# Where the sums of the output projection's weights and rows are formed: GpSimd inside the last two attention runs, VectorE beside the products

## The chip, the cores and the metric

The kernel runs on one core of one Trainium2 chip. The metric is the device time of one execution in microseconds. The kernel before was timed three times: 1077.59, 1077.86 and 1077.87 us, median 1077.86 us. One more execution was taken with the profiler; its time was 1078.45 us and its span in the trace 1076.5 us, so 1.95 us lie outside the span. All start times below count from the start of that span.

## The reference

One layer of a bidirectional encoder over 2048 tokens of width 1024. The token grid is 32 rows of 64 columns; attention is two-dimensional neighbourhood attention (8 rows by 16 columns around a query) with a learned bias per head.

```python
h = rmsnorm(x, norm_0)
proj = h @ w_in_0                      # (2048, 1024) @ (1024, 4096)
q, k, v, gate = jnp.split(proj, 4, axis=-1)
o = neighbourhood_attention(q, k, v, rpb_0)    # 16 heads of 64
x = x + (o * jax.nn.silu(gate)) @ w_out_0      # (2048, 1024) @ (1024, 1024)
return rmsnorm(x, norm_f)
```

Everything is float32. A product is made of three matmuls on a high part and a low part of each operand: high by high, high by low, low by high. Forming the parts of a 128x512 tile takes a copy on ScalarE (the high part, rounded) and a subtraction on VectorE (the low part).

## The kernel before, in words

**Stages.** First come the projections of v, q, k and the gate. Then 32 attention runs follow (16 heads in 8 pairs, by 4 blocks of 8 grid rows), with projection work and later the first output tiles fed between them as filler for TensorE. In run m the kernel normalises and transposes the weights of attention of run m-1, issues the scores of run m and then the products with v of run m-1. The loop goes to m = 32, where no new scores are issued. After it the rest of the output projection runs alone, and only this end of the program, from about 935 us on, is touched by the change.

**The output projection.** The 16 row tiles of 128 tokens are the result's units. Tiles 0 to 7 are made plainly, inside the runs (matmuls of lines 1332 to 1336). Tiles 8 to 15 are made in four pairs, (8,9), (10,11), (12,13) and (15,14), after the runs, in `rows_by_seven`: a pair of row tiles and the two halves of K and of the output columns form a 2x2 by 2x2 block product, done in seven block products instead of eight (Winograd's form of Strassen's scheme). This needs sums of blocks on both sides:

- weights: T1, T2, T3 and T4 from the four quarters B11, B12, B21, B22 of `w_out`. `land_first` and `land_rest` load the quarters again as raw tiles (16 DMAs, line 1354), `sum_T1` and `sums_T23` form T1 to T3 on GpSimd (lines 1369, 1373, 1374), `sum_T4` on VectorE (1378), and `split_quarter` makes their high and low parts (ScalarE 1389, VectorE 1390).
- rows: for each pair A11, A12, A21, A22 are loaded by `load_rows_of` (line 1401). `sum_rows` forms S1 to S4 on GpSimd (line 1413), and `form_rows` makes high and low parts (ScalarE 1406, VectorE 1407).

**The seven products.** Each product is 12 matmuls 128x128 by 128x512 (line 1432). The order in a pair is P1, P6, P2, P7, P5, P4, P3; for the first two pairs P1 and P2 of both are put in front: P1(8,9), P1(10,11), P2(8,9), P2(10,11), then the other five of the first pair, then of the second. Products share PSUM banks: P2 adds onto the bank of P1, P7 and P4 onto that of P6, P3 onto that of P5. So P2 must wait until ScalarE has copied P1 out (line 1437), P7 until VectorE has read P6 (line 1442), P4 until VectorE has read P7 (1442), P3 until VectorE has read P5 (line 1213). GpSimd adds the residual rows to some of these intermediate tiles (lines 1445, 1449).

**Closing a row tile.** `add_rows` adds the residual (1213), `square` sums squares on ScalarE (1216), `finish` takes the root and scales: inside the runs the root is a polynomial of eight small VectorE instructions (1236 to 1243), after the runs VectorE, ScalarE's square root and VectorE again (1231 to 1234); then two multiplications on VectorE (1251) and two stores (1255). The last tile, 15, has its own form (1199 to 1209, 1227, 1247, 1248).

**What sets the order.** The order on each engine is the order in which the program issues instructions; each engine works through its own queue strictly in that order. All loads and most stores are issued by SyncE's queue, also in order. A clock counted in matmuls (`due`, `store`, `later`) decides when a deferred step is issued; in `rows_by_seven` the table `todo` attaches loads, sums and splits to the index of a product.

## Time and profile before

| what | value |
|---|---|
| median of three timed runs | 1077.86 us |
| the profiled execution | 1078.45 us, span 1076.5 us, mean granted clock 0.985 |
| TensorE busy (matmuls) | 1045.8 us, 97% |
| VectorE busy | 733.3 us, 68% |
| ScalarE busy | 556.1 us, 52% |
| GpSimd busy | 312.9 us, 29% |
| last matmul of the attention products ends | 965.35 us |
| last matmul of all ends | 1068.88 us |

How to read it: a timeline row gives start, duration, engine, line, operation, output and input tiles, count, and in brackets how long the engine had been idle and which instruction released it. A row with a count merges neighbours: its duration is from the first start to the last end. In a stretch view "PEclk" is the TensorE clock that was granted, 1.00 being full speed. Matmul ends overlap the next start, so the pace of matmuls is read from their starts.

### The profile page before, as it was taken

The page shows a single profiled execution, that of the slowest core. Times are in us where ns is not written, and L with a number is a line of the kernel's source. Part 1 is how long each engine was busy: PE and PEld are TensorE (multiplying, and loading weights), DVE is VectorE, ACT ScalarE, POOL GpSimd, SP SyncE. Part 2 cuts the span into 40 slices and gives each one's busy share as a digit, 9 for nine tenths or more (in the row PEclk, how much of TensorE's full clock was granted, in tenths as well). Part 3 has the DMA queues.
Part 4 walks back from the last instruction along what each step waited for, and adds up shares of the span by engine and source line. Part 5 has one row for each costly group of instructions (what it writes and reads, how often), then busy time and mean ns, then how long its engine had stood idle before and what let it go on. Part 6 is the DMA issues. An engine that isn't in the chain of part 4 may idle for free. (4 is left out here: it accounts for less than half of the span.)

```text
span 1076.5 us, 20235 instructions
## 1 busy us (share of the span) xinstructions
PE 1045.8 (97%) x7268; PEld 854.9 (79%) x7268; DVE 733.3 (68%) x1569; ACT 556.1 (52%) x1299; POOL 312.9 (29%) x382
## 2 busy tenths in 40 slices
PE   9999999999999999999999999999999999995896
PEld 6888888887888888888887888888887888874685
DVE  5475667768897535564656665777877877679566
ACT  7645233434453333333323777787887766554233
POOL 0000312212220000000003677665654322264462
PEclk9999999999999999999999999999999999987899
DMA  9634444444455334342327778778776897781542
GB/s 315 213 98 130 131 139 136 130 136 148 147 166 147 89 88 122 94 127 99 117 87 242 234 237 251 216 260 241 250 236 208 257 300 258 243 276 53 166 137 78
DMA packets 123708, 188.51 MB, mean 175 GB/s; under 512 B 11160, under 2 KB 55448, under 8 KB 123608
## 3 DMA queue, kind: packets, MB, share of 16 engines
q1 hardware_dynamic: 123176, 186.83, 55.6%
q8 instruction: 57, 0.93, 0.3%
q10 hardware_dynamic: 432, 0.40, 0.1%
q14 instruction: 43, 0.35, 0.1%
HBM read 136.85 MB, written 50.33 MB: 174 GB/s over the span
## 5 line engine op out<-in xcount | busy, mean ns | idle before, releaser
L436 PE MATMUL pp<-h,f 128*128 128x512 f32 x672 | 217.3, 389 | 0.0
L1042 ACT ACTIVATE x<-x,st 128x360 f32<-128x360 f32 (+5 forms) x256 | 151.2, 593 | 23.0 <-DVE st L1036 23.0
L436 PEld LDWEIGHTS pp<-h,f 128*128 128x128 f32 x672 | 126.1, 188 | 26.1
L1056 POOL TENSOR_SCALAR x<-x,st 128x480 f32<-128x480 f32 (+5 forms) x192 | 112.2, 602 | 117.1 <-DVE st L1047 113.9
L436 PE MATMUL pp<-t,f 128*128 128x512 f32 x558 | 141.7, 389 | 0.1
L456 POOL TENSOR_TENSOR tmp<-tmp,rb 128x512 f32<-128x512 f32 x36 | 58.4, 1622 | 268.8 <-DVE tmp L454 233.4
L436 PE MATMUL pp<-l,f 128*128 128x512 f32 x336 | 130.7, 389 | 0.0
L996 POOL TENSOR_TENSOR em<-e,mk 128x264 f32<-128x264 f32 (+3 forms) x64 | 50.9, 827 | 260.3 <-DMA mk<-in_masks_dram 246.8
L1036 DVE CUSTOM_DVE_ANT_0 x<-s,em 128x360 f32<-128x360 f32 (+5 forms) x256 | 122.9, 535 | 0.0
L436 PEld LDWEIGHTS pp<-t,f 128*128 128x128 f32 x558 | 104.7, 188 | 22.3 <-DVE u L449 0.6
L419 DVE TENSOR_TENSOR f<-raw,f 128x512 fp32r<-128x512 f32 x105 | 76.5, 729 | 43.6 <-ACT f L418 43.5
L1028 PE MATMUL s<-kt,q 64*128 64x480 f32 (+5 forms) x512 | 94.6, 487 | 0.3 <-ACT k L366 0.3
L1135 PEld LDWEIGHTS o<-pta,vt 120*64 120x64 f32 (+2 forms) x1792 | 81.8, 138 | 16.1 <-DVE st L1036 13.6
L560 PE MATMUL pv<-wh,h 128*128 128x512 f32 x256 | 88.4, 390 | 0.7 <-ACT h L521 0.4
L1135 PE MATMUL o<-pta,vt 120*64 120x128 f32 (+5 forms) x1792 | 86.4, 254 | 2.2 <-ACT pta L1089 1.8
L560 PE MATMUL pv<-wl,h 128*128 128x512 f32 x256 | 88.2, 390 | 0.0
L560 PE MATMUL pv<-wh,l 128*128 128x512 f32 x256 | 88.1, 389 | 0.0
L1028 PEld LDWEIGHTS s<-kt,q 64*128 64x128 f32 x512 | 64.9, 186 | 15.8 <-DVE pta L1089 1.1
L418 ACT ACTIVATE f<-raw 128x512 fp32r<-128x512 f32 x105 | 63.7, 624 | 26.5 <-PE pp L436 12.5
L1089 DVE COPY pta<-ph 120x512 f32<-120x512 f32 (+5 forms) x96 | 56.9, 639 | 29.6 <-PE ph L1113 29.5
L436 PEld LDWEIGHTS pp<-l,f 128*128 128x128 f32 x336 | 63.1, 188 | 13.2
L1089 ACT ACTIVATE pta<-ph 120x512 f32<-120x512 f32 (+5 forms) x96 | 49.6, 557 | 38.0 <-PE ph L1113 37.3
(192 smaller groups left out, 1903.4 us busy)
## 6 DMA issues: line engine op xcount, KB each, us to landing
raw<-in_wg_dram SPq DMA_DIRECT2D x124, 256.0 KB, 4.3
row<-in_xr_dram SPq DMA_DIRECT2D x32, 256.0 KB, 4.2
vd<-v SPq DMA_DIRECT2D x32, 256.0 KB, 2.6
sgd<-sg SPq DMA_DIRECT2D x32, 256.0 KB, 2.4
q<-qd SPq DMA_DIRECT2D x32, 256.0 KB, 5.5
sgt<-sgd SPq DMA_DIRECT2D x32, 256.0 KB, 6.2
xr<-in_x_dram SPq DMA_DIRECT2D x32, 256.0 KB, 5.1
ogd<-og SPq DMA_DIRECT2D x32, 256.0 KB, 3.3
```

The source lines that it names most:

```text
L418: nc.scalar.activation(t[:, 0], src, AF.Copy)
L419: nc.vector.tensor_tensor(t[:, 1], src, t[:, 0].bitcast(F32), OP.subtract)
L436: nc.tensor.matmul(B[n, P], t[:, int(m == 2), c], x[k][int(m == 1)], start=P in (1, 6, 5) and k == 0 and m == 0, stop=k == 3 and m == 2, s ...
L456: nc.gpsimd.tensor_tensor(tmp, tmp, rb[c], OP.mult)
L560: nc.tensor.matmul(ps[t], a[:, o], b, start=k == 0 and m == 0, stop=k == NK - 1 and m == 2)
L996: (nc.gpsimd if attending[0] or not s else nc.vector).tensor_tensor(sh(t), E[p, s][:, u0 + 4:u1 + 4, v0 + 8:v1 + 8].rearrange("p u (s v) - ...
L1028: nc.tensor.matmul(pst[s], qt[a, qs], kt[a, :r1 - r0, c0:c1].rearrange("p r (s c) -> p s r c", c=8), start=True, stop=True)
L1036: nc.vector.tensor_tensor_reduce(X[i, C][s], pst[s], EM[p, ROW_TYPE[T], COL_TYPE[C], s], -1.0, 1e38, OP.add, OP.min, st[:, o:o + 1])
L1042: nc.scalar.activation(X[i, C][s], X[i, C][s], AF.Exp, bias=st[:, o:o + 1], scale=-1.0, accum_out=st[:, 4 + o:5 + o])
L1056: nc.gpsimd.tensor_scalar(X[i, C][s], X[i, C][s], st[:, o:o + 1], 1.0, op0=OP.mult, op1=OP.mult)
L1089: (nc.vector.tensor_copy if h else lambda o, i_: nc.scalar.activation(o, i_, AF.Copy))(t[:k, h, b * 512:b * 512 + w], banks_[b, h][:k, :w])
L1135: nc.tensor.matmul(to.rearrange("d (h q) -> d h q", q=64) if nq > 64 else to, vt[:k, strip, s * 64:s * 64 + 64], t[:k, h, at:at + 64] if n ...
```

## The change

The constant `PLAIN` stays 8, so that in the new code `E` is 2 and the order of the products, and of all matmuls, is as before. What differs:

1. **Weights' sums.** One more raw quarter (B22's third) is loaded with the first ten, and all eleven are issued in one go in run 31, not one after another over several matmuls. `sum_T1` is issued in run 31 before its scores; the first two of the eight T2/T3 sums at the end of run 31, the other six in run 32 where all twelve stood. All are still on GpSimd.
2. **Rows' loads.** A11 and A12 of the first two pairs are loaded in run 31 instead of 32; the other row and residual loads are placed anew in `todo`.
3. **First splits.** The high and low parts for P1 of the two first pairs are issued before the transposes of run 32, those for P2 after them, where before all four stood after.
4. **Rows' sums** S1 to S4 move from GpSimd to VectorE for all four pairs; S4 overwrites S2 and not A12.
5. **Splits of T1, T3, T4 and the T4 sum** are issued after the fourth, first, sixth and first product; before, T3 and the T4 sum stood ahead of all products, T1 after the first and T4 after the second.
6. **Roots.** Tile 7, whose root came after the runs, now takes the polynomial form on VectorE; ScalarE's square root comes first with tile 9.
7. **Tile 14** is multiplied by the final norm's weights before its root is known, like tile 15, and scaled by ScalarE and VectorE half each.

```diff
+        if n == tiles - 2:
+            w = ev([128, 512], F32, "yw")
+            nc.vector.scalar_tensor_tensor(w, y, 0.5 ** 0.5 / NF_SCALE, late["nf"][j], op0=OP.mult, op1=OP.mult)
+            Y[n][0][j] = w
         store(("y", n, j), 5, square)
...
-            if ended[0]:
+            if n >= PLAIN:
                 nc.vector.tensor_scalar(h, st[:, 0:1], st[:, 1:2], 0.5 * D * EPS, op0=OP.add, op1=OP.add)
                 nc.scalar.activation(h, h, AF.Sqrt)
                 nc.vector.reciprocal(r, h)
-                nc.vector.tensor_scalar(r, r, 0.5 ** 0.5 / NF_SCALE, None, op0=OP.mult)
+                if n < tiles - 2:
+                    nc.vector.tensor_scalar(r, r, 0.5 ** 0.5 / NF_SCALE, None, op0=OP.mult)
                 return
...
-            if n == tiles - 1:
+            if n >= tiles - 2:
                 nc.scalar.activation(y[0], y[0], AF.Copy, scale=r)
                 nc.vector.tensor_scalar(y[1], y[1], r, None, op0=OP.mult)
...
-            store(("y", n), 24, scale)
+            store(("y", n), 12 if n == tiles - 2 else 24, scale)
...
-        which = [(f, k) for f in ("B12", "B11") for k in range(4)] + [("B22", 0), ("B22", 1)]
+        which = [(f, k) for f in ("B12", "B11") for k in range(4)] + [("B22", k) for k in range(3)]
...
-        A[m, f] = xp([128, 512], F32, "s") if f in ("S1", "S2") else A[m, {"S3": "A21", "S4": "A12"}[f]]
-        nc.gpsimd.tensor_tensor(A[m, f], A[m, a], A[m, b], o)
+        A[m, f] = xp([128, 512], F32, "s") if f in ("S1", "S2") else A[m, {"S3": "A21", "S4": "S2"}[f]]
+        nc.vector.tensor_tensor(A[m, f], A[m, a], A[m, b], o)
...
-            U[m, 1] = ep([128, 512], F32, "p1")
+            U[m, 1] = (xp if m == 2 else ep)([128, 512], F32, "p1")
...
-        for f in ("S1", "S2", "S3", "S4"):
-            sum_rows(0, f)
-        sum_T4()
+        for f in ("A21", "A22"):
+            load_rows_of(0, f)
+        for m in range(E):
+            load_rest_of(m, 0, 0)
         split_quarter("T2", [a[k, 1] for k in range(4) for a in (woh, wol)])
         sixth = sixths()
-        split_quarter("T3", [fresh(lp)] + [fresh(vh)] * 2 + [fresh(sp)] + sixth[:4])
         for i, (m, P) in enumerate(seq):
             rows_product(m, P)
             if i == 0:
+                sum_T4()
+                split_quarter("T3", [fresh(lp)] + [fresh(vh)] * 2 + [fresh(sp)] + sixth[:4])
+            if i == 3:
                 spot = mkp([128, 3, 512], F32R, "t1")
                 split_quarter("T1", [spot[:, j] for j in range(3)] + [fresh(kp, 960)] + sixth[4:6] + [fresh(vh)] * 2)
-            if i == 1:
+            if i == 5:
                 split_quarter("T4", [fresh(mp)] * 6 + [fresh(kp, 960), fresh(mp)])
...
-            later_loads(land_first(), 1, 0.7)
+            later_loads([lambda: [f() for f in land_first()]], 1.5, 0)
+            later_loads([lambda f=f, i=i: load_rows_of(i, f) for i in ((2, 0, 1) if PLAIN <= 6 else (0, 1)) for f in ("A11", "A12")], 10, 0.5)
         if m == cycles:
             later_loads([land_rest], 4, 0)
-            later_loads([lambda f=f, i=i: load_rows_of(i, f) for f in ("A11", "A12") for i in range(2)], 6, 0.5)
-            later_loads([lambda f=f: load_rows_of(0, f) for f in ("A21", "A22")], 10, 0.5)
...
             if m == cycles:
-                sum_T1()
-                sums_T23(range(2))
-                sums_T23(range(2, 4))
+                sums_T23(range(1, 4))
...
+        if m == cycles:
+            for n in range(3 if PLAIN <= 6 else 2):
+                form_rows(n, 1)
         sums = next_sums(m) == m + 1
         if m:
             turns(m - 1)
...
-            for s in ((0, 1), (1, 1), (0, 2), (1, 2)):
-                form_rows(*s)
+            for n in range(3 if PLAIN <= 6 else 2):
+                form_rows(n, 2)
         else:
+            if m == cycles - 1:
+                sum_T1()
             scores(2 * m)
...
             values(2 * m - 2)
             values(2 * m - 1)
+        if m == cycles - 1:
+            sums_T23((0,))
```

More of the change, by code (lines that the diff above doesn't have):

```diff
@@ L1358, in land_first @@
         homes = [spot[:, i] for i in range(3)] + [kp([128, 960], F32, "land")[:, :512]]
-        homes += [mp([128, 512], F32, "land") for _ in range(4)] + [qp([128, 512], F32, "land"), sp([128, 512], F32, "land")]
-        which = [(f, k) for f in ("B12", "B11") for k in range(4)] + [("B22", 0), ("B22", 1)]
+        homes += [mp([128, 512], F32, "land") for _ in range(4)] + [p([128, 512], F32, "land") for p in (qp, sp, lp)]
+        which = [(f, k) for f in ("B12", "B11") for k in range(4)] + [("B22", k) for k in range(3)]
         return [lambda w=w, h=h: load_quarter(*w, h) for w, h in zip(which, homes)]
     def land_rest():
-        for w in [("B22", 2), ("B22", 3)] + [("B21", k) for k in range(4)]:
+        for w in [("B22", 3)] + [("B21", k) for k in range(4)]:
             load_quarter(*w, mp([128, 512], F32, "land"))
@@ L1462, in rows_by_seven @@
             TF[f] = [(woh[4 * r + k, c], wol[4 * r + k, c]) for k in range(4)]
-        seq = [(0, 1), (1, 1), (0, 2), (1, 2)] + [(m, P) for m in (0, 1) for P in order7 if P not in (1, 2)]
-        seq += [(m, P) for m in range(2, len(PAIRS)) for P in order7]
+        E = 3 if PLAIN <= 6 else 2
+        seq = [(m, P) for P in (1, 2) for m in range(E)] + [(m, P) for m in range(E) for P in order7 if P not in (1, 2)]
+        seq += [(m, P) for m in range(E, len(PAIRS)) for P in order7]
         at = {s: i for i, s in enumerate(seq)}
@@ L1471, in rows_by_seven @@
         for i, s in enumerate(seq):
-            if i >= 4:
+            if i >= 2 * E:
                 on(i - 3, form_rows, *s)
         for m in range(len(PAIRS)):
-            s = at[m, 6] if m < 2 else at[m, 1]
-            first = s - (5 if m == 1 else 7)
-            if m:
-                if m == 1:
-                    names = ((first, "A21"), (first, "A22"))
-                else:
-                    names = ((first, "A21"), (first, "A22"), (first + 2, "A11"), (first + 3, "A12"))
-                for i, f in names:
-                    on(i, load_rows_of, m, f)
-                for i, f in ((2, "S1"), (2, "S2"), (2, "S3"), (3, "S4")) if m == 1 else ((4, "S1"), (4, "S2"), (5, "S3"), (7, "S4")):
-                    on(first + i, sum_rows, m, f)
-            for d, j, k in ((-2, 0, 1), (-2, 0, 0), (-1, 1, 1), (0, 1, 0)):
-                if m > 1:
-                    on(s + d, load_rest_of, m, j, k)
-                elif (j, k) != (0, 0) and (m, j, k) != (0, 0, 1):
-                    on(s + d, load_rest_of, m, j, k)
-        for f in ("S1", "S2", "S3", "S4"):
-            sum_rows(0, f)
-        sum_T4()
+            s = at[m, 6] - (m >= E)
+            loads = {0: (), 1: ((-7, "A21"), (-6, "A22")), 2: ((-7, "A21"), (-6, "A22"), (-6, "A11"), (-6, "A12"))}
+            for d, f in loads.get(m, ((-7, "A21"), (-7, "A22"), (-6, "A11"), (-4, "A12"))):
+                on(s + d, load_rows_of, m, f)
+            for d, f in ((-4, "S1"), (-4, "S2"), (-3 if m < E else -2, "S3"), (-2 if m < E else -1, "S4")):
+                on(s + d, sum_rows, m, f)
+            rest = ((-3, 1, 0), (-2, 0, 1), (-1, 1, 1)) if m == 0 else ((-3, 1, 0), (-3, 0, 1), (-2, 1, 1)) if m < E else                 ((-2, 0, 1), (-2, 0, 0), (-1, 1, 0), (0, 1, 1))
+            for d, j, k in rest:
+                on(s + d, load_rest_of, m, j, k)
+        for f in ("A21", "A22"):
+            load_rows_of(0, f)
+        for m in range(E):
+            load_rest_of(m, 0, 0)
         split_quarter("T2", [a[k, 1] for k in range(4) for a in (woh, wol)])
         sixth = sixths()
-        split_quarter("T3", [fresh(lp)] + [fresh(vh)] * 2 + [fresh(sp)] + sixth[:4])
         for i, (m, P) in enumerate(seq):
@@ L1653, in build @@
         due(1)
-    for e in ((0, 0, 0), (1, 0, 0), (0, 0, 1)):
-        load_rest_of(*e)
     rows_by_seven()
```

## The prediction

> **What bounds the kernel now.** I read the page's slices first: TensorE is at nine tenths nearly everywhere, except in slice 37 of 40, and its granted clock sinks there too.

> ```profile
> PE   9999999999999999999999999999999999995896
> ...
> PEclk9999999999999999999999999999999999987899
> ```

> Then the stretch view for TensorE alone (columns: stretch, length, busy, count, PEclk, DMA share, GB/s), the timelines of TensorE, ScalarE and GpSimd, and VectorE's.

> ```profile
> 959.00:963.00 4.00, 1.85 (x42) 1.00 0.96 305
> 963.00:970.00 7.00, 6.79 (x46) 0.52 0.90 333
> ...
> 977.00:986.00 9.00, 0.00 (x0) 0.50 0.00 0
> 986.00:990.00 4.00, 3.69 (x9) 0.50 0.00 0
> ...
> 1011.00:1015.00 4.00, 0.48 (x3) 0.94 0.47 169
> 1015.00:1021.00 6.00, 5.79 (x14) 0.50 0.50 171
> ```
> ```profile
> 961.18 0.66 PE L1135 MATMUL o<-pta,vt 96*64 96x128 f32 x8 [1.79 <-ACT pta L1089]
> 962.20 3.15 PE L1135 MATMUL o<-pta,vt 96*64 96x64 f32 x48 [0.36 <-DVE pta L1089]
> 965.56 0.80 PE L1432 MATMUL py<-woh,f 128*128 128x512 f32 x1 [0.21 <-ACT f L1406]
> ...
> 986.31 0.80 PE L1432 MATMUL py<-woh,f 128*128 128x512 f32 x1 [12.74 <-ACT p L1437]
> ...
> 997.63 1.61 PE L1432 MATMUL py<-t,f 128*128 128x512 f32 x6 [0.88 <-DVE u L1442]
> ...
> 1015.21 2.90 PE L1432 MATMUL py<-t,f 128*128 128x512 f32 x6 [3.73 <-ACT f L1406]
> ...
> 1020.46 1.95 PE L1432 MATMUL py<-t,f 128*128 128x512 f32 x6
> ...
> 1022.94 3.57 PE L1432 MATMUL py<-t,f 128*128 128x512 f32 x15
> ...
> 1026.35 0.39 PE L1432 MATMUL py<-woh,f 128*128 128x512 f32 x1
> ...
> 1068.49 0.39 PE L1432 MATMUL py<-woh,f 128*128 128x512 f32 x1
> ```
> ```profile
> 974.53 1.71 POOL L1413 TENSOR_TENSOR s<-raw 128x512 f32<-128x512 f32 x1
> ```
> ```profile
> 977.33 1.28 ACT L1232 ACT_TABLE_LOAD   x1
> 985.57 0.20 ACT L1232 ACTIVATE st<-st 128x1 f32<-128x1 f32 x1 [6.96 <-DVE st L1231]
> 985.68 0.58 ACT L1437 ACTIVATE p<-py 128x512 f32<-128x512 f32 x1
> ```

> After two products TensorE stands still for 12.74 us. P2 needs ScalarE's copy of P1 (L1437). That copy stood behind a square root which waited 6.96 us for VectorE, and VectorE was busy with twelve sums and splits that had waited for GpSimd, done with the weights' sums only at 974.53. A second standstill, 3.73 us, lies ahead of P7 of the second pair. After each the clock is at half for 4 to 6 us. From 1022.94 to 1026.35 fifteen matmuls start, 0.227 us each, 2.73 a product; the 336 matmuls of the four pairs would take 76.4 us at that pace and took 1068.88 - 965.56 = 103.3. So at most some 27 us can be gained in the products.

> **The change part by part.** The order on each engine follows from the diff; the matmuls' order is unchanged.

> *T1 sums in run 31.*

> ```profile
> 952.75 3.39 POOL L1056 TENSOR_SCALAR x<-x,st 128x288 f32<-128x288 f32 x6 [10.26 <-DVE st L1047]
> 956.10 5.00 POOL L1369 TENSOR_TENSOR land<-land 128x512 f32<-128x512 f32 x4
> ```
> ```profile
> L1354 SPq DMA_DIRECT2D land<-in_w_out_dram x16: 327/432/1475, 937.8 to 958.1; - x16
> ...
> DMA to landing us min/median/max: 3.5/5.3/7.8
> ```

> Four sums, 5.00 us, move into GpSimd's 10.26 us of idleness before 952.75. The eight quarters they need are issued from 937.8 on at about 0.5 us each, so the last lands near 941.8 + 5.3 = 947; the sums end by 949 to 951. Cost nothing. SyncE issues the store of the attention output and the load of v behind six more quarters, some 4 us later, but v is used only at 961. If landings took 7.8 us, the cover is just gone and the normalising starts about 1 us late.

> *Two sums between the normalisings.*

> ```profile
> 957.96 1.43 PE L1113 MATMUL ph<-ident,x 64*96 64x64 f32 x44
> ```

> One T2 and one T3 sum come after four of the six scalings, 2 x 1.25 us. The last two scalings end near 958.7, not 956.14 (952.75 + 3.39). The transposes that need them are the second half of this group, so TensorE loses 0 to 0.7 us; I take 0.1.

> *Two row splits ahead of the copies out of the transposes.*

> ```profile
> 960.41 1.74 DVE L1089 COPY pta<-ph 96x512 f32<-96x512 f32 x3
> ...
> 965.54 6.21 DVE L1407 TENSOR_TENSOR f<-raw,f 128x512 fp32r<-128x512 f32 x4 [0.54 <-ACT f L1406]
> ...
> 994.32 0.68 DVE L1407 TENSOR_TENSOR f<-raw,f 128x512 fp32r<-128x512 f32 x1
> 994.92 0.68 DVE L1213 TENSOR_TENSOR y<-py,xr 128x512 f32<-128x512 f32 x1
> ```
> ```profile
> L1243 DVE SCALAR_TENSOR_TENSOR st<-st x7: 159/159/1197, 838.8 to 958.7; 128x1 f32<-128x1 f32 x7
> ```

> With GpSimd silent a 128x512 VectorE instruction is followed by the next after 0.60 us (994.32 to 994.92); beside GpSimd's sums the splits took 1.55 each, and a 128x1 instruction 1.20 where its median is 0.16. The copies out of PSUM did not suffer (0.58 each). The two splits are issued while GpSimd still works on the six sums: 3.1 us. So the three copies end near 965.5, where 962.15 was. The 48 matmuls that need them then run wholly at half clock (before, partly): about 3.9 us, not 3.15. **The first product starts at 969.5, 3.9 us later than now.** Bounds 1 us (GpSimd late, VectorE gets through first) and 5 us.

> *The 12.74 us go.* Ahead of the copy of P1 ScalarE now has only splits whose sources are ready by 968. The 48 leading matmuls run in one piece: ten at half clock (0.43 us), 38 at 0.227, to about 982.4, and P6 to 985.1; now P6 ends at 996.75 (997.63 less the 0.88 of idleness behind it).

> *What is late next: VectorE.* P7 waits for VectorE to read P6 (L1442), and in VectorE's order that stands behind all of this, from 965.5:

> ```profile
> 992.39 1.41 DVE L1251 SCALAR_TENSOR_TENSOR y<-y,st,acc 128x512 f32<-128x512 f32 x2
> ```

> Two scalings beside GpSimd's last sums, 2.5, and two splits 1.2; the attention output, which waits for the products with v, to 970.1; four T2 splits 2.4; the polynomial root 1.8; four T4 sums 2.4; four T3 splits 2.4; three row sums 1.9 and a split 0.7 (P6's, ready at 981.7, in time); two scalings 1.4; four single instructions 2.4; four T1 splits 2.4; a split 0.6; the reading 0.7. That ends at 989.2. **P7 starts at 989.3 instead of 997.63; a 4.2 us standstill stays, and I gain 8.3 here.** A standstill of that length brings half clock (2.15 of 4 us idle did at 959 to 963): 2.0 us lost, bounds 0 and 3. P7 ends at 994.0 (now 997.63 + 2.73 = 1000.36).

> *Second pair.* From 994.0 VectorE has 14 instructions at 0.60, to 1002.5. Then comes tile 9's root, now with the 1.28 us table load inside it, to 1004.0; two singles, two scalings, another root 0.8, and the reading of P6, to 1008.0. TensorE has four products (10.9) and is at 1005.2. So P7 waits about 3 us (now 3.73), and half clock again costs 2.6 (now 1020.46 - 1015.21 - 2.73 = 2.5). The next product starts at 1013.4, now at 1020.46: 7.1 us ahead.

> *Row sums on VectorE, pairs three and four.*

> ```profile
> 1030.00:1050.00 20.00, 19.80 (x88) 15.99 (x87) 13.87 (x24) 7.37 (x19) 10.51 (x7) 1.00 0.41 132
> ```
> ```profile
> 1031.04 2.44 DVE L1251 SCALAR_TENSOR_TENSOR y<-y,st,acc 128x512 f32<-128x512 f32 x2
> ```

> VectorE (third busy figure) is at 13.87 of 20 us; four sums a pair add 2.4 of 19.1, and contention with GpSimd's sums goes. VectorE stays below TensorE. Ahead of P7's release stands one sum more, 0.6, while the two scalings that took 2.44 beside such a sum take 1.4. The 17 products from 1020.46 took 48.4 us, 46.4 at full pace; I take 46.9. Bounds 46.4 and, if each sum is exposed, +5. The last matmul ends at 1060.3, 8.6 us earlier.

> *The tail.*

> ```profile
> 1070.65 1.41 DVE L1251 SCALAR_TENSOR_TENSOR y<-y,st,acc 128x512 f32<-128x512 f32 x2
> 1071.97 0.16 DVE L1228 RECIPROCAL st<-st 128x1 f32<-128x1 f32 x1
> ...
> 1072.16 0.72 ACT L1247 ACTIVATE yw<-yw,st 128x512 f32<-128x512 f32 x1 [1.55 <-DVE st L1228]
> ```

> Tile 14's two scalings stand before the last reciprocal. In the new order one half goes to ScalarE and the other fits ahead of the last PSUM read, so the reciprocal comes 1.2 us earlier (bounds 0.7 and 2, as fewer stores land together).

> **Sum**: 8.6 + 1.2 = 9.8, less 0.1 = 9.7 us. The profiled execution, 1078.45 us (span 1076.5 and 1.95 around it), would become 1068.75. It lies 0.59 above the median of 1077.86, so I say **1068.2 us**.

> [...]

> **Rivals.**

> ```profile
> 995.00:1000.00 5.00, 4.12 (x19) 3.12 (x18) 2.58 (x4) 2.40 (x7) 1.67 (x1) 1.00 0.78 222
> ```
> ```profile
> DVE f L1407 <- ACT f L1406: 7.5, 7, 3.5
> ```

> - *The clock holds at the second pair's P7.* As the idle 0.88 us at 996.75 left it at full (PEclk 1.00 from 995 to 1000), 3 us may too, if they fall across two intervals of whatever the clock looks at. 2.6 us less: 1065.6. Chance 0.12. [...]
> - *Full relief*: the products run on from 969.5 without a wait, 76.4 + 2.3 for the cold start = 1048.2; the tail now 7.6, then 6.4, span 1054.6, time 1056. It needs VectorE to read P6 right away, against the count of instructions above. Chance 0.07.
> - *Half-exposed row sums*: the four sums of each of the last two pairs stand in front of readings, 2.4 us a pair: 1073. For it: VectorE's splits already wait for ScalarE's, seven times, once for 3.5 us. Chance 0.12.
> - *Slower: VectorE becomes the bound in pairs three and four.* Its work of 13.25 + 2.4 us a pair is under TensorE's 19.1, but what it waits for inside its order (ScalarE's splits, roots) comes on top. If those waits pass 3.5 us a pair, P7 stands still, and each stop cools the clock (2.6). From stops of 2.3 us on the two pairs give back all 9.7 us; stops of 3 us give 11.2 and 1079.4 (bounds 1078 to 1083). Against it: part of what VectorE waits for now is GpSimd (the 2.44 above), and that goes. Chance 0.05.
> - *The change does not do what it says*: the early sums wait for their quarters and end no sooner than 974.5, and VectorE's queue is as late as now: 1077.9. The landings above (947) speak against it. Chance 0.02.

> **How the numbers follow.** The forecast has 0.62. Its own range, with the bounds of front, clock and tail, is 1064.5 to 1072. Adding the two neighbours gives 1062.5 to 1074.5, which holds some 0.84. About 0.2% (2 us) is what a measurement can tell here. Faster: 0.62 + 0.12 + 0.07 + 0.12 = 0.93; same 0.02; slower 0.05.

> **What would show it.** Right: no wait on L1437 in front of P2; a first product near 969.5; a wait of about 4 us before the first pair's P7, released by VectorE's L1442 instruction, and one of about 3 us before the second pair's; half clock behind both; no wait over 0.5 us in pairs three and four; the last reciprocal right behind the last premultiplication. Wrong: transposes that start late in run 32; the first P7 starting before 986 or after 993; VectorE waits for row DMAs behind stores in SyncE's queue.

## The result and the profile after

The kernel after takes 1068.9 us (median of 4 runs: 1067.17, 1067.71, 1070.1, 1070.8), the kernel before 1077.78 us in the same comparison. The ratio is 0.9918, interval 0.9898 to 0.9938: 8.9 us less. The profiled execution is the one of 1067.17 us, with a span of 1065.3 us and a mean granted clock of 0.991. It is the fastest of the four, so gains read from its trace are larger than the 8.9 us between the medians.

The slices of the page of after, TensorE busy:

```profile
PE   9999999999999999999999999999999999997797
```

The one weak slice of before, at five tenths, has become two at seven tenths. TensorE's timeline of after, the rows behind a wait and some between them:

```profile
956.95 1.55 PE L1113 MATMUL ph<-ident,x 64*96 64x64 f32 x44
961.80 5.12 PE L1135 MATMUL o<-pta,vt 96*64 96x128 f32 x56 [3.29 <-ACT woh L1394]
966.85 0.80 PE L1437 MATMUL py<-woh,f 128*128 128x512 f32 x1
...
977.63 0.50 PE L1437 MATMUL py<-woh,f 128*128 128x512 f32 x1 [0.47 <-ACT p L1442]
...
988.27 2.90 PE L1437 MATMUL py<-t,f 128*128 128x512 f32 x6 [4.85 <-ACT t L1394]
...
992.50 1.53 PE L1437 MATMUL py<-t,f 128*128 128x512 f32 x6
...
1000.66 0.47 PE L1437 MATMUL py<-woh,f 128*128 128x512 f32 x1 [1.81 <-DVE y L1213]
...
1009.38 1.62 PE L1437 MATMUL py<-t,f 128*128 128x512 f32 x6 [1.38 <-ACT f L1411]
...
1012.23 1.52 PE L1437 MATMUL py<-t,f 128*128 128x512 f32 x6
...
1058.83 0.39 PE L1437 MATMUL py<-woh,f 128*128 128x512 f32 x1
```

Line numbers behind the edits are five higher than before: the matmul is L1437, the copy of P1 L1442, VectorE's readings L1447, the row splits L1411 and L1412, the weights' splits L1394 and L1395.

The last transposes of run 32 (L1113) start at 956.95; before, they started at 957.96. Run 31 and what lies ahead of it differ by about this much from one execution to the next (with the same code up to there the transposes start at 956.95 in after, 957.06 in e4, 957.24 in e2 and 957.82 in e1), so I put the two timelines on one scale by adding 1.01 to after:

| step | before | after, plus 1.01 | gain |
|---|---|---|---|
| first product starts | 965.56 | 967.86 | -2.3 |
| P7 of the first pair starts | 997.63 | 989.28 | 8.3 |
| P7 of the second pair starts | 1015.21 | 1010.39 | 4.8 |
| the product behind it starts | 1020.46 | 1013.24 | 7.2 |
| last matmul starts | 1068.49 | 1059.84 | 8.65 |
| span ends | 1076.5 | 1066.31 | 10.2 |

The stop of 12.74 us in front of the first P2 is gone; 0.47 us are left in front of the second. What is left over 0.5 us in the products are three stops, 4.85, 1.81 and 1.38 us, all in the first two pairs, each ended by work that VectorE does in its own order. VectorE's timeline of after:

```profile
957.56 0.68 DVE L1213 TENSOR_TENSOR y<-po,xr 128x512 f32<-128x512 f32 x1
958.16 2.94 DVE L1412 TENSOR_TENSOR f<-raw,f 128x512 fp32r<-128x512 f32 x2
961.02 1.74 DVE L1089 COPY pta<-ph 96x512 f32<-96x512 f32 x3
962.68 3.44 DVE L1256 SCALAR_TENSOR_TENSOR y<-y,st,acc 128x512 f32<-128x512 f32 x2
966.05 2.35 DVE L1412 TENSOR_TENSOR f<-raw,f 128x512 fp32r<-128x512 f32 x2
...
968.93 2.48 DVE L1395 TENSOR_TENSOR wol<-land,woh 128x512 fp32r<-128x512 f32 x4
...
984.43 1.28 DVE L1395 TENSOR_TENSOR t<-land,t 128x512 fp32r<-128x512 f32 x2
...
987.43 0.69 DVE L1447 TENSOR_TENSOR u<-py,p 128x512 f32<-128x512 f32 x1
...
993.31 4.67 DVE L1395 TENSOR_TENSOR t<-land,t 128x512 fp32r<-128x512 f32 x4
...
999.83 0.68 DVE L1213 TENSOR_TENSOR y<-py,u 128x512 f32<-128x512 f32 x1
...
1004.62 0.16 DVE L1237 RECIPROCAL st<-st 128x1 f32<-128x1 f32 x1 [0.98 <-ACT st L1236]
...
1008.56 0.68 DVE L1447 TENSOR_TENSOR u<-py,p 128x512 f32<-128x512 f32 x1
```

The reading of P6 (L1447) ends at 988.12, and P7 starts at 988.27. The trace puts this wait down to ScalarE's weight split L1394; the one that came last by its time is the reading, behind four T1 splits that begin at 984.43. (In e9 and e10 below P7 starts 0.15 and 0.14 us behind the reading's end, in after 0.15.) P3's start at 1000.66 follows the reading of P5 at 999.83, behind four T4 splits that took 4.67 us beside GpSimd. The second P7, at 1009.38, follows the reading at 1008.56, which stands behind two roots; the first of them waits 0.98 us for ScalarE.

### The profile page after: what moved, and what is told of

Its sections match the earlier page's. It is cut to its first block, busy times and chain, and to the rows that moved or that the text cites. A ratio compares the mean times of both kernels' runs of the same rounds, so it can differ in the third digit from the quotient of the medians.

```text
span 1065.3 us, 20217 instructions
## 1 busy us (share of the span) xinstructions
PE 1045.1 (98%) x7268; PEld 855.0 (80%) x7268; DVE 737.2 (69%) x1590; ACT 556.1 (52%) x1299; POOL 288.5 (27%) x366
## 4 chain that ended last, share of the span: by engine, by line
PE 90%; DVE 5%; ACT 1%; DMA 1%; issue 1%; SPq 0%; DVEq 0%; ACTq 0%
PE pp L436 36%; PE pv L560 16%; PE s L1028 8%; PE o L1135 7%; PE py L1437 6%; PE ph L1113 4%; PE po L1337 2%; PE pp L382 2%; PE po L1341 2%; PE po L1339 2%; PE pp L384 2%; PE pp L380 2%; DVE y L1256 1%; DMA out_dram<-y 1%; DMA vt<-vd 0%
## 5 line engine op out<-in xcount | busy, mean ns | idle before, releaser
L1056 POOL TENSOR_SCALAR x<-x,st 128x480 f32<-128x480 f32 (+5 forms) x192 | 112.2, 601 | 107.5 <-DVE st L1047 104.4
L1135 PEld LDWEIGHTS o<-pta,vt 120*64 120x64 f32 (+2 forms) x1792 | 83.0, 140 | 17.3 <-DVE st L1036 13.6
L1135 PE MATMUL o<-pta,vt 120*64 120x128 f32 (+5 forms) x1792 | 87.8, 256 | 3.3 <-ACT woh L1394 3.3
L1089 DVE COPY pta<-ph 120x512 f32<-120x512 f32 (+5 forms) x96 | 56.9, 639 | 29.6 <-PE ph L1113 29.5
L1089 ACT ACTIVATE pta<-ph 120x512 f32<-120x512 f32 (+5 forms) x96 | 49.6, 557 | 37.1 <-PE ph L1113 36.3
```

The costliest lines, as they stand in the source:

```text
L1056: nc.gpsimd.tensor_scalar(X[i, C][s], X[i, C][s], st[:, o:o + 1], 1.0, op0=OP.mult, op1=OP.mult)
L1089: (nc.vector.tensor_copy if h else lambda o, i_: nc.scalar.activation(o, i_, AF.Copy))(t[:k, h, b * 512:b * 512 + w], banks_[b, h][:k, :w])
L1135: nc.tensor.matmul(to.rearrange("d (h q) -> d h q", q=64) if nq > 64 else to, vt[:k, strip, s * 64:s * 64 + 64], t[:k, h, at:at + 64] if n ...
```

## The experiments

**Theory**: once the weights' sums are early, the order of VectorE's work decides when both P7 and P3 start, and TensorE stands still until then; half clock behind a stop is paid on top. **Rivals**: the first product's start is what is passed on to the end (the two splits ahead of the copies then cost their time); a single part of the change, the early sums or the order, makes the whole gain; the loads decide.

### The early sums alone: e5_early_sums_only

The kernel before, with the eleven quarters issued in one go, T1's sums in run 31 and the first two of the others at its end; the rest as before.

```diff
-        which = [(f, k) for f in ("B12", "B11") for k in range(4)] + [("B22", 0), ("B22", 1)]
+        which = [(f, k) for f in ("B12", "B11") for k in range(4)] + [("B22", k) for k in range(3)]
...
-            later_loads(land_first(), 1, 0.7)
+            later_loads([lambda: [f() for f in land_first()]], 1.5, 0)
...
-                sum_T1()
-                sums_T23(range(2))
-                sums_T23(range(2, 4))
+                sums_T23(range(1, 4))
...
+            if m == cycles - 1:
+                sum_T1()
...
+        if m == cycles - 1:
+            sums_T23((0,))
```

> The kernel before with one part of the change: the eleven quarters loaded in one go in run 31, and the sums T1, T2 and T3 issued earlier on GpSimd as in the change; every other order as before. Theory (the standstill of 12.74 us had two causes in a row, GpSimd's late sums and a queue of splits and a root ahead of ScalarE's copy of P1): GpSimd ends near 974 with the row sums, VectorE passes the splits of T3 near 980, the copy comes near 981 instead of 985.7, and the standstill falls to some 7 to 8 us: 1072 to 1074.5 us. Rival (GpSimd's lateness was the whole cause): the standstill goes, 1067 to 1069 us.

Measured: 1073.84 us (1073.43 to 1074.29), ratio 0.9965 [0.9952, 0.9978], within the theory's range. TensorE's timeline:

```profile
982.31 0.80 PE L1432 MATMUL py<-woh,f 128*128 128x512 f32 x1 [8.81 <-ACT p L1437]
...
994.03 1.61 PE L1432 MATMUL py<-t,f 128*128 128x512 f32 x6 [0.88 <-DVE u L1442]
```

The stop in front of P2 is 8.81 instead of 12.74 us. Up to the start of the second P7 everything behind it keeps its form (the waits ahead of the two P7 are 0.88 and 3.73 us, as before), shifted by 3.6 us. So the early sums alone give some 3.8 us.

### The order alone: e6_order_only

The kernel before, with T4's sum and T3's splits behind the first product, T1's behind the fourth, T4's behind the sixth, and tile 7's root in the polynomial form. The weights' and rows' sums stay late and on GpSimd.

```diff
-            if ended[0]:
+            if n >= PLAIN:
...
-        sum_T4()
...
-        split_quarter("T3", [fresh(lp)] + [fresh(vh)] * 2 + [fresh(sp)] + sixth[:4])
         for i, (m, P) in enumerate(seq):
             rows_product(m, P)
             if i == 0:
+                sum_T4()
+                split_quarter("T3", [fresh(lp)] + [fresh(vh)] * 2 + [fresh(sp)] + sixth[:4])
+            if i == 3:
...
-            if i == 1:
+            if i == 5:
...
```

> The kernel before with another part of the change: the sum of T4 and the splits of T3, T1 and T4 issued behind the first, the fourth and the sixth product, and tile 7's root as a polynomial on VectorE; all sums late and on GpSimd as before. Theory: the copy of P1 comes near 975.5 and P2 starts 10 us earlier, but P7 waits for VectorE's reading of P6 near 993.5 in place of 997.5, with a cold clock: the gain is only 2 to 4 us, 1074 to 1076 us. Rival (the queue ahead of the copy was the whole cause): 1067 to 1069 us.

Measured: 1078.5 us (1074.73 to 1079.4, 10 runs), ratio 1.0002 [0.9993, 1.0011]. Both expectations missed. TensorE's timeline, and VectorE's:

```profile
975.42 0.50 PE L1432 MATMUL py<-woh,f 128*128 128x512 f32 x1 [2.10 <-ACT p L1437]
...
994.34 2.90 PE L1432 MATMUL py<-t,f 128*128 128x512 f32 x6 [2.39 <-DVE u L1442]
...
1016.86 2.68 PE L1432 MATMUL py<-t,f 128*128 128x512 f32 x6 [2.50 <-ACT f L1406]
```
```profile
1000.44 5.76 DVE L1390 TENSOR_TENSOR t<-land,t 128x512 fp32r<-128x512 f32 x4
```

The 12.74 us in front of P2 are gone (2.10; 4.08 us are lost inside P6 instead), and the first P7 starts 3.3 us earlier than before, as the theory has it. But P7 now runs at half clock: six of its matmuls take 2.90 us, in before 1.61, and all twelve 5.25 instead of 2.81. That takes 2.4 of the 3.3 us back at once. The rest, and more, goes to the four T4 splits, which VectorE had done during the long stop and which now stand behind P7, where GpSimd adds residual rows and forms row sums: they take 5.76 us. P3 waits 1.64 us, the second P7 2.50 us, and it starts at 1016.86 where before had 1015.21. So a long stop had given VectorE time for work that is due all the same, and the shorter one, 2.39 us here, is followed by half clock too. Early sums alone 3.8, order alone nothing: together with the rest they make 8.9, so the parts do not add up one by one.

### The tail alone: e3_tail_only

The kernel before, with tile 14 multiplied by the norm's weights ahead of its root and scaled by ScalarE and VectorE half each.

```diff
+        if n == tiles - 2:
+            w = ev([128, 512], F32, "yw")
+            nc.vector.scalar_tensor_tensor(w, y, 0.5 ** 0.5 / NF_SCALE, late["nf"][j], op0=OP.mult, op1=OP.mult)
...
-            if n == tiles - 1:
+            if n >= tiles - 2:
...
```

> The kernel before with the tail edit alone (tile 14 multiplied by the final norm's weights ahead of its root and scaled half by ScalarE, half by VectorE). Theory: the last reciprocal no longer stands behind two 0.70 us scalings, so the end comes 1.2 us earlier: 1076.6 us. Rival: the landing of the last stores sets the end whatever VectorE does: 1077.8 us.

Measured: 1076.65 us (1075.51 to 1078.62, 10 runs), ratio 0.9989 [0.9979, 0.9998]. That is 1.2 us less, with an interval from 0.2 to 2.3: as the theory has it, though the interval nearly reaches the rival's nothing.

### The row sums back on GpSimd: e1_rows_gpsimd

```diff
-        nc.vector.tensor_tensor(A[m, f], A[m, a], A[m, b], o)
+        nc.gpsimd.tensor_tensor(A[m, f], A[m, a], A[m, b], o)
```

> The changed kernel with one edit: the row sums S1 to S4 are back on GpSimd, at their new places. Theory (VectorE's order is the bound ahead of the first pair's P7, and a GpSimd sum blocks a two-input VectorE instruction for longer than the 0.60 us that VectorE needs for the sum itself): each GpSimd sum beside VectorE's splits costs it about 1.0 us and saves 0.6; P7 of the first pair starts 0 to 2 us later, and splits of later pairs wait for GpSimd again: 1069.5 to 1072 us against the changed kernel's 1068.9. Rival (VectorE is relieved by 1.9 us ahead of that P7 and by 2.4 us in each later pair): 1066 to 1067 us.

Measured: 1068.26 us (1068.01 to 1068.31), ratio 0.9908 [0.9894, 0.9923], not to be told from after. Neither expectation holds. TensorE's timeline:

```profile
990.46 1.62 PE L1437 MATMUL py<-t,f 128*128 128x512 f32 x6 [1.97 <-DVE u L1447]
```

The transposes start at 957.82 here, so the first P7 is 1.3 us later than in after (990.46 - 957.82 = 32.64, against 31.32). That much the theory had right. But the stop fell into two pieces, 3.14 us ahead of the second P2 and 1.97 ahead of P7, and P7 ran at full clock: six of its matmuls took 1.62 us, in after 2.90. Which engine forms the row sums is worth nothing measurable here; in these two executions the 1.3 us that VectorE gains are paid back in clock.

### The splits behind the transposes again: e7_splits_behind

```diff
-        if m == cycles:
-            for n in range(3 if PLAIN <= 6 else 2):
-                form_rows(n, 1)
...
-            for n in range(3 if PLAIN <= 6 else 2):
-                form_rows(n, 2)
+            for P in (1, 2):
+                for n in range(2):
+                    form_rows(n, P)
```

> The changed kernel with one edit: the two row splits for the first products are issued behind the transposes again, together with those for P2. Theory (VectorE's total up to its reading of P6 sets P7, not the start of the first product): the products with v run about 3 us earlier, the first product 1 to 2 us earlier, and P7 starts where it does now; time 1068 to 1070 us as the changed kernel's. Rival (the later start of the first product, which the prediction charged with 3.9 us, is paid for at the end): 1066 to 1067 us.

Measured: 1068.24 us (1067.71 to 1069.51), ratio 0.9915 [0.9899, 0.9932]. TensorE's timeline:

```profile
958.07 1.51 PE L1113 MATMUL ph<-ident,x 64*96 64x64 f32 x44
...
963.19 0.50 PE L1437 MATMUL py<-woh,f 128*128 128x512 f32 x1
...
989.40 2.90 PE L1437 MATMUL py<-t,f 128*128 128x512 f32 x6 [3.33 <-ACT t L1394]
```

The first product starts 5.1 us behind the transposes' start, in after 9.9 us behind. The 4.8 us are all given back at the next waits (1.68 us behind the first two matmuls, 5.18 ahead of the second P2, 3.33 ahead of P7; in after none, 0.47 and 4.85): the first P7 comes 31.33 us behind the transposes, in after 31.32. This is the plainest evidence that VectorE's order sets P7, and that the first product's start is not passed on.

### T1's splits one product later: e2_t1_later

```diff
-            if i == 3:
+            if i == 4:
                 spot = mkp([128, 3, 512], F32R, "t1")
```

> The changed kernel with one edit: the four splits of T1 are issued after the fifth product, behind VectorE's reading of P6, and not after the fourth. Theory (that reading stands in VectorE's order behind work that nobody needs yet): P7 of the first pair starts about 2.4 us earlier in the trace, its standstill falls from 4.85 to about 2.4 us, and P5 still finds T1 ready: 1065.5 to 1067 us, less if the clock then stays up. Rival (the standstill only moves on to P5, which needs T1): P7 earlier, but P5 waits 2 us, and the time stays at 1068 to 1070 us.

Measured: 1065.89 us (1064.38 to 1066.32), ratio 0.9884 [0.987, 0.9899]: 3.7 us below the 1069.59 of after in the same comparison (e4), within the theory's range. TensorE's timeline:

```profile
986.14 1.93 PE L1437 MATMUL py<-t,f 128*128 128x512 f32 x6 [2.42 <-ACT t L1394]
...
1006.95 2.20 PE L1437 MATMUL py<-t,f 128*128 128x512 f32 x6 [2.62 <-ACT f L1411]
```

Four splits of 0.60 us fewer in front of the reading, and the stop is 2.42 instead of 4.85 us: 2.4 each time. How much of the 3.7 us is this stop and how much the clock is not settled: counted from the start of the transposes (957.24), the last matmul starts 1.1 us earlier than in after's profiled execution and 3.3 us earlier than in that of e4.

### The same kernel again: e4_after_again

No edit.

> The changed kernel once more, unedited, to see where its spread of 3.6 us between executions comes from (the kernel before spread over 0.3 us). Theory: the standstills that are left are about as long as the stretch over which the clock looks at TensorE, so in one execution a standstill is followed by half clock and in the next it isn't; a second profile then shows the same order and the same waits, but half clock at other places, and the times lie between 1067 and 1071 us. Rival: the spread comes from landings of the row and weight loads, and the two profiles differ in waits for DMA.

Measured: 1069.59 us (1067.33 to 1070.21), ratio 0.9917 [0.9903, 0.9932]; the profiled execution took 1069.5 us, 2.3 us more than after's, though the transposes start 0.1 us behind after's (957.06). The stretch views for TensorE, first after, then e4 (columns: stretch, length, busy, count, PEclk, DMA share, GB/s), and e4's timeline at the second P7:

```profile
987.90:991.30 3.40, 3.03 (x7) 0.50 0.31 85
998.10:1001.50 3.40, 1.59 (x8) 1.00 0.00 0
1001.50:1004.90 3.40, 3.40 (x10) 0.50 0.52 143
1008.30:1011.70 3.40, 2.31 (x10) 1.00 0.34 132
1022.00:1060.00 38.00, 37.18 (x163) 1.00 0.26 90
```
```profile
986.90:990.30 3.40, 1.94 (x5) 0.50 0.37 126
990.30:993.70 3.40, 3.40 (x10) 0.50 0.71 224
1007.40:1010.80 3.40, 0.80 (x4) 0.99 0.40 154
1010.80:1014.20 3.40, 3.40 (x10) 0.51 0.31 119
```
```profile
1010.14 2.38 PE L1437 MATMUL py<-t,f 128*128 128x512 f32 x6 [2.60 <-ACT f L1411]
```

Behind 955 us the stretches at half clock in eight of the traces (before, after, e1, e2, e4, e8, e9 and e10) are one to four times 3.4 us long (four in before, around the stop of 12.74 us), and in one execution they begin and end on one grid of that step. The grid does not lie the same in every execution: the first of these stretches begins at 960.6 in after and at 963.0 in e4, 3.6 and 5.9 us behind the start of the transposes. In after it cuts so that P7's start (988.27) lies early in a cold stretch, which holds 3.03 us of work, and the next is at full clock. In e4 the stretch holds only 1.94 us of work, and a second cold one follows. The stops themselves are almost the same (P7 at 988.36). In these two executions the clock makes the difference: the twelve matmuls of the first P7 take 5.26 us in e4 and 4.23 in after, those of the second 1014.56 - 1010.14 = 4.42 and 1012.23 - 1009.38 = 2.85; that is 2.6 us, of which 0.4 come back because P3 ran at full clock in e4. The rival is out: these 2.2 us are nearly all of the 2.3, neither trace marks a wait of TensorE for a DMA behind 950 us, and after's marks none of VectorE, ScalarE or GpSimd. So the loads do not decide here either. Whether the clock also makes the rest of the 3.6 us between the four runs of after is not shown, as only one of them was profiled. (The runs of before lay within 0.3 us in the first comparisons, but up to 3.0 us apart in the later ones.)

### Work for TensorE during the stop: e8_filler_matmuls

Fourteen matmuls into a bank that nothing reads, right behind P6 of the first pair; they are not part of the reference.

```diff
+            if (m, P) == (0, 6):
+                idle = bank(512, "pd")
+                for i in range(14):
+                    nc.tensor.matmul(idle, t[:, 0, 0:128], TF[f][0][0], start=True, stop=True)
```

> The changed kernel with 14 extra matmuls into a bank that nobody reads, right behind P6 of the first pair, inside the standstill of 4.85 us; the results are untouched. Theory (a standstill costs twice, once as idleness and once as half clock behind it): the filler takes 3.2 us of the standstill, P7 starts where it does now but runs at full clock, and what follows is 1.5 to 2.5 us earlier: 1066.5 to 1067.5 us. Rival (VectorE sets the pace behind it anyway): 1068.5 to 1070 us.

Measured: 1067.01 us (1066.19 to 1067.64), ratio 0.9901 [0.9887, 0.9916], within the theory's range, though the interval overlaps that of after. TensorE's timeline:

```profile
988.74 1.62 PE L1437 MATMUL py<-t,f 128*128 128x512 f32 x6 [1.70 <-ACT t L1394]
...
991.56 1.52 PE L1437 MATMUL py<-t,f 128*128 128x512 f32 x6
```

P7 starts no earlier (the transposes start at 957.42, 0.47 later than in after), but its twelve matmuls take 991.56 - 988.74 = 2.82 us instead of 992.50 - 988.27 = 4.23. Half clock behind the first stop costs 1.4 us, and that comes on top of the stop: counted from the transposes, the last matmul too starts 1.4 us earlier than in after (100.46 us against 101.88).

### Towards a better version: e9, e10, e11

e9 is e2 with ScalarE's table for the square root loaded ahead of time:

```diff
+        warm = tiny.tile([128, 8], F32, name="warm")
+        nc.scalar.activation(warm[:, 0:1], ones[:, 0:1], AF.Sqrt)
         split_quarter("T2", [a[k, 1] for k in range(4) for a in (woh, wol)])
...
-            if i == 3:
+            if i == 4:
```

> The kernel after with T1's splits one product later (as e2, 1065.89 us) and ScalarE's table for the square root loaded 20 us ahead, by a root of one column of ones before T2's splits, so that tile 9's root does not carry the 1.28 us load. Theory: the second pair's P7 (wait of 2.6 us in e2) stands behind this root in VectorE's order; it starts about 1.3 us earlier, and the time is 1064.3 to 1065.4 us. Rival: the wait ends by ScalarE's own splits or by VectorE's splits beside GpSimd, and the root is not late; then the time stays at 1065.5 to 1066.3 us and the wait at 2.3 us or more.

Measured: 1064.68 us (1063.74 to 1065.35), ratio 0.988 [0.9864, 0.9897] against 1077.31: within the theory's range, and the lowest median of this study, though its interval overlaps e2's. TensorE's timeline of e9 at the second P7, and VectorE's ahead of it:

```profile
1007.10 1.62 PE L1437 MATMUL py<-t,f 128*128 128x512 f32 x6 [1.43 <-ACT f L1411]
...
1009.94 1.52 PE L1437 MATMUL py<-t,f 128*128 128x512 f32 x6
```
```profile
1002.99 0.69 DVE L1213 TENSOR_TENSOR y<-py,u 128x512 f32<-128x512 f32 x1 [1.01 <-PE py L1437]
```

The time is the theory's, but not the way to it. VectorE waits 0.27 us for the root (0.98 in after), but then 1.01 us for P3, which ran at half clock in this execution (granted clock 0.54 from 998.90 to 1002.30). So the second P7 starts at 1007.10, no earlier than e2's 1006.95; its wait is shorter (1.43 instead of 2.62) because TensorE came later, and with the shorter wait P7 stayed at full clock (1.62 us for six matmuls, in e2 2.20). How much of the 1.2 us between the medians is the table and how much the grid stays open.

e10 is e9 with the second pair's row sums one product later and the scalings of the roots that end inside the products deferred:

```diff
-            store(("y", n), 18, scale)
-            store(("y", n), 36, send)
+            store(("y", n), 54 if ended[0] else 18, scale)
+            store(("y", n), 72 if ended[0] else 36, send)
...
-            for d, f in ((-4, "S1"), (-4, "S2"), (-3 if m < E else -2, "S3"), (-2 if m < E else -1, "S4")):
+            for d, f in ((-4 + (m == 1), "S1"), (-4 + (m == 1), "S2"), (-3 + (m == 1) if m < E else -2, "S3"), (-2 + (m == 1) if m < E else -1, "S4")):
```

> As e9, and two things more are moved away from VectorE's order ahead of the second pair's P7: the second pair's four row sums stand one product later, and the two scalings of each root that ends inside the products run at a lag of 54 instead of 18 steps (their store at 72 instead of 36). Theory: what stands in front of the readings of P6 sets both standstills, and each 0.6 us taken out of VectorE's order ahead of them comes back whole: P7 of the second pair waits under 1.5 us, and the time is 1062.5 to 1064.5 us. Rival: the sums and scalings are then late for P3, P4 or the stores, and waits appear there of the same size: 1064.5 to 1066.5 us.

Measured: 1067.56 us (1067.3 to 1067.78), ratio 0.9908 [0.9893, 0.9923]: above both expectations, nearer to the rival. TensorE's, GpSimd's and VectorE's timelines of e10:

```profile
985.31 1.62 PE L1437 MATMUL py<-t,f 128*128 128x512 f32 x6 [1.15 <-ACT t L1394]
...
1007.49 2.90 PE L1437 MATMUL py<-t,f 128*128 128x512 f32 x6 [5.31 <-ACT f L1411]
...
1012.74 1.83 PE L1437 MATMUL py<-t,f 128*128 128x512 f32 x6
```
```profile
985.25 1.29 POOL L1450 TENSOR_TENSOR u<-u,xr 128x512 f32<-128x512 f32 x1 [17.22 <-DVE u L1447]
991.50 4.06 POOL L1450 TENSOR_TENSOR u<-u,xr 128x512 f32<-128x512 f32 x1 [4.96 <-DVE u L1447]
```
```profile
995.59 0.69 DVE L1213 TENSOR_TENSOR y<-py,u 128x512 f32<-128x512 f32 x1 [1.16 <-POOL u L1450]
```

The first pair is faster: P7 starts 1.0 us and P3 (996.43) 2.0 us earlier than in e9 (986.33 and 998.38), though the transposes start 0.3 us later (957.73, 957.45). But the second P7 is not. VectorE, freed at one place, waits at the next: 1.16 us for GpSimd's sum, which took 4.06 us beside VectorE's four splits, then 0.70 us, at 998.77, for a split of ScalarE that needs a row sum now one product later. All that TensorE has won it waits off in one piece, 5.31 us, and after it the clock is at half: P7 takes 1012.74 - 1007.49 = 5.25 us, in e9 1009.94 - 1007.10 = 2.84. These 2.4 us, with 0.4 of the later start, are the 2.8 us between the two spans (1065.9 and 1063.1).

e11 is e10 with eight such filler matmuls as in e8 behind P6 of the first pair:

```diff
+                for i in range(8):
+                    nc.tensor.matmul(idle, t[:, 0, 0:128], TF[f][0][0], start=True, stop=True)
```

> As e10, with eight matmuls of 128x512 into a bank that nothing reads, right behind P6 of tiles 8 and 9, where TensorE stands still for about 2.4 us (work that is not the reference's and changes none of its outputs). Theory: the clock stays at full over the first pair's P7 and the time is 0.5 to 1.9 us below e10's. Rival: a standstill of 2.4 us leaves the clock at full in most executions, and eight matmuls only delay what follows: within 0.4 us of e10's, or above it.

Measured: 1067.14 us (1066.42 to 1067.88), ratio 0.9904 [0.989, 0.9919]: about 0.4 us below e10, with ranges that overlap, as the rival has it. The wait ahead of the second P7 is 5.33 us, as in e10. A stop of 1.15 us had not cooled the clock in e10 (six matmuls of P7 in 1.62 us), so filling it gives nothing that can be told; the stop that costs is the other one.

## Why the prediction was right, step by step

The forecast was 1068.2 us and the likeliest case came: 1068.9 us, and 1069.59 when the same kernel was run again. The sum holds because its large terms hold: the long stop goes, VectorE sets the next one, the last two pairs lose nothing, and the tail gives 1.2 us. Two agreements within 0.2 us, at the first P7 and behind the second, are partly luck, as errors cancel there.

**T1's sums in run 31, cost 0: right.** GpSimd's timeline of after:

```profile
946.10 4.98 POOL L1374 TENSOR_TENSOR land<-land 128x512 f32<-128x512 f32 x4 [4.62 <-DMA land<-in_w_out_dram]
951.75 2.12 POOL L1056 TENSOR_SCALAR x<-x,st 128x288 f32<-128x288 f32 x4 [0.67 <-DVE st L1047]
```

The sums end at 951.08, 0.67 us before the normalising: hidden, with little to spare.

**The sums between the normalisings, 0.1 us: right.** The transposes take 1.55 us instead of 1.43.

**Two splits ahead of the copies, first product 3.9 us later: the size was off.** The splits took 2.94 us, near the 3.1 forecast, but VectorE's root chain had ended 1.2 us sooner (the sum behind it starts at 957.56 + 1.01 = 958.57, before at 959.81), so the product starts 2.3 us later, not 3.9. And e7, without this delay, ends no earlier: it is not passed on. In the prediction's sum TensorE's 985.1 did not count either, as VectorE's 989.2 is the later; but the late product stood in VectorE's own count, which waits for the products with v until 970.1 (see the next step but one).

**No wait in front of P2: not quite.** A wait of 0.47 us is there (2.58 in the profiled execution of e4): it lies in front of the second P2, as ScalarE's second copy of P1 stands behind splits of T3. VectorE sets P7 anyway, so it costs nothing.

**VectorE is next, P7 of the first pair at 989.3, a stop of 4.2 us: right, the exact start with luck.** On before's scale P7 starts at 989.28, after a stop of 4.85. From the T2 splits (L1395, 968.93) on, the count of instructions by 0.60 us each, from one row pair of the trace, holds: 968.93 to 988.12 is 19.19 us, forecast 970.1 to 989.2, that is 19.1. That VectorE came to these splits on time is luck. Its copies ended at 962.76 + 1.01 = 963.77 and not at 965.5, and the two scalings and two splits behind them took 968.33 - 962.68 = 5.65 us beside GpSimd's last sums, not 3.7; it did not wait for the products with v. e2 shows the cause: four splits taken from in front of the reading take 2.4 us from the stop. e7 and e8 show that neither the first product nor the clock moves P7's start.

**Second pair, a wait of 3 us at P7 and half clock: two errors that cancel.** The next product starts at 1013.24, forecast 1013.4. But P7 itself starts at 1010.39, where the forecast implies 1013.4 - 2.73 - 2.6 = 1008.1. The wait is in two pieces: 1.81 us ahead of P3, which the prediction did not have, and 1.38 us ahead of P7. What it missed is the four T4 splits, which it put at 0.60 us each; beside GpSimd's two residual sums they took 4.67 us for four, 1.17 each, and the reading that releases P3 is behind them. The half clock then fell on P3 and not on P7, which took 2.85 us instead of 5.3 and so made up for its late start. That is luck of the execution: in e4's, P7 does run at half clock, and the next product starts at 1014.56 + 0.90 = 1015.46 on before's scale, 2.1 us behind the forecast. (A slip in the sum changes nothing: TensorE's four products from 994.0 end at 1004.9, not 1005.2, and VectorE's 1008.0 is later than both.)

**Row sums on VectorE, pairs three and four without loss: right.** The timeline marks no wait behind 1012; TensorE is busy for 37.18 of 38 us at full clock. The rival that VectorE becomes the bound there is refuted, and so is half-exposure.

**The tail, 1.2 us: right.** From the last matmul's start to the span's end 8.0 us before, 6.5 after; e3 gives 1.2 by itself. VectorE's timeline of after, at the end:

```profile
1060.38 0.68 DVE L1209 SCALAR_TENSOR_TENSOR yw<-y,acc 128x512 f32<-128x512 f32 x1
1060.98 0.16 DVE L1232 RECIPROCAL st<-st 128x1 f32<-128x1 f32 x1
```

The last reciprocal stands right behind the last premultiplication, as forecast.

**The clock as a rival.** The prediction gave a chance of 0.12 to a clock that holds at the second pair's P7. In the profiled execution of after it held there (six matmuls in 1.62 us) but had cooled at P3, so the 2.6 us of that rival were not won; in that of e4 it cooled at P7. So it is no property of the kernel but of where the grid lies, and a count of instructions could not have given the 2.3 us between these executions.

**What stays open.** Why run 31 ends up to 0.9 us earlier in some executions of the same code was not tried, nor whether the grid's place is the whole of the spread. The early sums and the new order without the rest of the change were not run either; e1 and e7 show only that the row sums on VectorE and the two splits ahead of the copies add nothing that can be measured.

## What to carry to other kernels

When a long wait goes, ask what the engine behind it did with that time: here the early sums alone gave 3.8 us and the order alone nothing, in part because the stop had served VectorE to do work that was due anyway, in part because the shorter stop, 2.39 us in e6, was followed by half clock as well. Count the instructions in front of the next reading in that engine's queue, each at its uncontended or contended price: 19.1 us of such a count came out within 0.1 us, while four splits beside GpSimd, counted at the uncontended price as 2.4 us, took 4.67. A stop can cost twice, by itself and by the half clock behind it (1.4 us in e8's comparison), but half clock is free where another engine is late anyway: the first nine matmuls of the products ran at half clock in after (966.85 to 970.8) and at full clock in e4 (from 966.67 on), and P7 started 31.3 us behind the transposes in both.

## What the runs showed of the hardware

**Contention of VectorE and GpSimd goes both ways.** Beside GpSimd's two sums four VectorE splits took 4.67 us (after, from 993.31), where four took 2.48 with GpSimd idle (after, from 968.93). In e10 four such splits took 2.48 us (from 991.35), and GpSimd's one sum beside them 4.06 us, where such a sum took 1.29 earlier in the same execution (from 985.25, beside two splits that took 2.42). In both cases with four splits the first split starts some 0.15 us ahead of GpSimd's sum (993.31 and 993.47 in after, 991.35 and 991.50 in e10), and once VectorE is slowed, once GpSimd. What decides it was not shown.
